# Copied bias rows laid out by partition, and the recurrent parameters loaded as rows and worked out earlier

## The chip, the cores and the metric

The kernel runs on one core of a Trainium2 chip. The metric is the device time of one execution in microseconds (us). Its engines are named as in the profile: PE (TensorE, matrix products; PEld is its weight load), DVE (VectorE), ACT (ScalarE), POOL (GpSimd) and SP (SyncE, which issues the transfers, DMAs). Each engine runs its own instructions in the order in which they were written; the engines wait for each other by semaphores.

## The reference

A row of 256 tokens of width 1024 goes through a first block of two layers and a second block. All is float32.

```python
# first block
for i in range(2):
    h = _multiscale_pool(...) if i == 0 else _diff_attention(...)      # 8 heads, relative position bias
    x = _layernorm(ALPHA * x + h, ...)
    x = _layernorm(ALPHA * x + (silu(x @ w_gate[i]) * (x @ w_up[i])) @ w_down[i], ...)
# second block
proj = rms_norm(x) @ w_in                                              # 1024 x 7752
y_a = moba_attention(...); y_b = dsa_attention(...)                    # 8 heads each, position bias
y_c = rg_lru(causal_depthwise_conv(xc, conv_w, conv_b), w_r, b_r, w_i, b_i, lam) * gelu(yc)
x = x + (sigmoid gates * (y_a @ w_pa, y_b @ w_pb, y_c @ w_pc), summed) @ w_o
x = x + square(relu(rms_norm(x) @ w_up)) @ w_down
return rms_norm(x)
```

The recurrent branch `rg_lru` needs eight vectors of 512 channels (four taps `conv_w`, `conv_b`, `b_r`, `b_i`, `lam`), and of the last one `softplus(-lam)`.

## The kernel before

**Products.** Each float32 operand is split exactly into a high and a low float32r part, and each product is three (high x high, low x high, high x low; lines 304 to 306, helper `mm3`). Weights come by units of 1 MB in two halves of 512 KB (`raw`); ACT casts a half to its high part (line 89), DVE subtracts to get the low part (line 98). Class `Stream` does this in the order of use: five raw halves may be in flight (`RAW_BUFS`), and a half is loaded when DVE has split the half five places before it. `Stream.step` issues such casts and splits after every block of products, so their place in ACT's and DVE's order is fixed when the program is written.

**Side work.** Class `Side` holds chains of short steps (Python generators). `tick`, after each block of 24 or 48 products, issues one step of each active chain, then a step of the stream. The attention heads (`diff_head`) are such chains.

**A feed-forward layer** (`ffn`) runs over eleven chunks of 256 hidden columns. From chunk 2 on a chunk is: 48 products for the gate (`proj_b`), SiLU on ACT (line 558), 48 for `up`, the multiplication on DVE (line 562), the split of the hidden chunk into `hh` (ACT, line 297) and `hl` (DVE, line 298), and then the down projection of the chunk before it into the banks `acc`, 24 products of 512 columns. The last three chunks do only token tile 0 there (12 products); what is due for tile 1 comes in `finish_layer`, which first completes tile 0 (12 products), issues its layer norm, does 24 + 6 products of tile 1 meanwhile, transposes tile 0 into `XTh`/`XTl` (line 373), and does the last 6. Small jobs hang on chunks by number (`aside`, a dictionary: chunk to function), issued after the chunk's products.

**What the change touches.** The position bias of 24 heads is worked out once as a table `R0` in DRAM (24 rows of 383 numbers). `spread_bias(h0)` copies four of these rows 128 times into `Rd` in DRAM, so that `load_bias(h0)` can read, for partition p, the row shifted by p. In the first feed-forward layer chunks 5 and 6 spread heads 0 to 7; in the second one chunks 5 to 8 spread heads 8 to 23. `load_rnn` (second feed-forward layer, chunk 2) loads the eight vectors with channels on partitions, four bytes a piece, into `cw` and `par`; `rnn_params` (chunk 9) works out `softplus(-lam)` by 27 DVE operations and one Exp on ACT, in one go; its results `sp8` are read in the recurrent branch of the second block.

Of the kernel before, what the change touches and what calls it, by code (L numbers as in the profile page):

```python
# [11 lines left out]
F32 = mybir.dt.float32  # L12
# [5 lines left out]
P = 128  # L18
# [19 lines left out]
# the merge of the branches, by blocks of 256 columns: gates (A, B, C), branches (a, b, c), output projection (O)  # L38
# [4 lines left out]
class Stream:  # L43
    """Weights in the order of use: DRAM -> SBUF by halves, each split exactly into a high and a low float32r part."""
# [7 lines left out]
    def load(self, n=None):  # L52
        """Issue loads of halves as far as buffers go, or up to the given count."""
        n = 2 * len(self.units) if n is None else n
        while self.n_dma < min(n, self.n_low + RAW_BUFS):
            i = self.n_dma
            src, (n_k, f) = self.units[i // 2]
            self.raw[i] = self.pool.tile([P, n_k // 2, f], F32, tag="raw", name=f"raw{i}", bufs=RAW_BUFS)
            self.nc.sync.dma_start(self.raw[i], src[:, i % 2 * (n_k // 2):(i % 2 + 1) * (n_k // 2)])
            self.n_dma += 1  # L60
# [42 lines left out]
    def step(self):  # L103
        """The low parts of halves whose high parts an earlier step issued, and the high part of the next half, or of
        two when there is room for two units."""
# [20 lines left out]
class Side:  # L126
    """Chains of short steps, emitted one step each after every block of products, so that their
    latencies pass while the tensor engine works."""
# [4 lines left out]
    def add(self, gen, delay=0, after=(), first=False):  # L133
        """delay: blocks to let pass, once the chains named in after have ended; first: ahead of others"""
# [6 lines left out]
    def tick(self, step=True):  # L141
        """step: of the stream too"""
# [16 lines left out]
def model_kernel(ctx: ExitStack, tc: tile.TileContext, a: dict, out: bass.AP, stop=None):  # L159
# [28 lines left out]
    # ---------------------------------------------------------------- inputs  # L188
# [15 lines left out]
    # -------------------------------------------------------- weight stream  # L204
# [10 lines left out]
    def u_spare(n):  # L215
        """the n-th unit from here goes to buffers that attention leaves free by then"""
        if n is not None:
            spare.add(len(units) + n)
# [42 lines left out]
    # weights of the pooling mix, in a buffer of the stream  # L261
# [17 lines left out]
    # ------------------------------------------------------------ constants  # L279
# [13 lines left out]
    # -------------------------------------------------------------- helpers  # L293
    def split_from(src, h, l, scale=None):
        """h + l = src exactly, both float32r; scale: a power of two or a per-partition column."""
# [12 lines left out]
    def proj_a(o, t, u, tick=True):  # L308
        """o[tok, cols] = X[tile t] @ W"""
# [9 lines left out]
    def proj_b(u, xT=None, n=256):  # L319
        """a bank [cols, j, tok] = (X @ W)^T"""  # L320
# [15 lines left out]
    def down(acc, t, parts, first, last, halves=(0, 1), tick=True):  # L336
        """acc[t][half] += hidden[tile t] @ W rows, for (hidden, unit) in parts"""
# [19 lines left out]
    def rsqrt(v, eps=None):  # L357
        """v[P, n] -> (v + eps) ** -0.5"""
# [21 lines left out]
    def ln(t, acc, g, b, scale=None, first=None, then=None):  # L380
        """first, then: other work, issued where the statistics are waited for"""
# [26 lines left out]
    def rms(t, squares, g):  # L408
        """x * g / rms(x), by halves; squares(h) issues the half's sum of squares and returns its column"""
# [8 lines left out]
    # the end of a layer for one tile: the vector work, then the transposes of the next layer's operand  # L418
# [31 lines left out]
    def finish_out(acc, g, own, late):  # L450
        """own: parts that complete tile 0; late: parts still due for tile 1"""
# [15 lines left out]
    def finish_layer(acc, end, own, late, n_next, quota):  # L467
        """own: parts that complete tile 0; late: parts still due for tile 1. Returns what remains of tile 1's end."""
# [98 lines left out]
    # rows of R0 hold, per head, 8 * bias at distance 255 - j (mask where j > 255); every partition's copy  # L567
    # of them, read at a row pitch one shorter, gives the bias of its query
    R0 = dr.tile([24, NREL], F32, name="R0")
    Rd = dr.tile([24, P, NREL], F32, name="Rd")  # L570
# [32 lines left out]
    def spread_bias(h0):  # L603
        load(Rd[h0:h0 + 4], R0[h0:h0 + 4][:, None, :].to_broadcast([4, P, NREL]))

    def load_bias(h0):
        """[q, head, k] with q of tile 1; columns 128.. serve tile 0"""
        bt = gen("bias", (4, T))
        load(bt, bass.AP(Rd_ap.tensor, Rd_ap.offset + h0 * P * NREL + 127, [[NREL - 1, P], [P * NREL, 4], [1, T]]))
        return bt  # L610

    # --------------------------------------------------- layer 0: pooling mix
    def pool_diff(t, h):
        """a half of (window mean - x)^T"""
# [68 lines left out]
    # ----------------------------------------------------- layer 0: feed forward  # L683
    gb1 = []

    def load_ln(g, b):
# [4 lines left out]
        5: lambda: spread_bias(0), 6: lambda: spread_bias(4)})  # L691
# [3 lines left out]
    # -------------------------------------------- layer 1: differential attention  # L695
# [25 lines left out]
    def proj_t():  # L721
        """a unit's columns, transposed, as float32 in SBUF"""
# [9 lines left out]
    def softmax(qT, kT, j, bias_of, out):  # L732
        """per map c (partitions 64c.. of qT and kT) [q of tile 0 x 128 keys | q of tile 1 x 256 keys]:
        exp(s - max), and the sums, column 2t + c"""
# [22 lines left out]
    def transpose3(src):  # L757
        """[keys, q of tile 0 | q of tile 1] for the first 128 keys, then [keys, q of tile 1] for the others"""
# [45 lines left out]
    v_proj(v, 3, pending)  # L804
    bias = [load_bias(0), load_bias(4)]
# [25 lines left out]
    # ----------------------------------------------------- layer 1: feed forward  # L831
    # parameters of the recurrent branch, channels on partitions: [128, 4]
    cw = sb.tile([P, 4, 4], F32, name="cw")
    par = sb.tile([P, 4, 4], F32, name="par")
    sp8 = sb.tile([P, 3, 4], F32, name="sp8")

    def load_rnn():
        def vec4(w):
            return w.rearrange("(c p) -> p c", p=P)

        for i in range(4):
            load(cw[:, i], vec4(a["conv_w_2"][0, i]))
        for i, n_ in enumerate(("conv_b_2", "b_r_2", "b_i_2", "lru_lambda_2")):
            load(par[:, i], vec4(a[n_][0]))

    def rnn_params():
        # softplus(-lam) = max(-lam, 0) + log1p(e), e = exp(-|lam|); log1p(e) = 2 atanh(e / (2 + e))
        lam = par[:, 3]
        nl, ab, e, z, z2, ser = (small(4) for _ in range(6))
        nc.vector.tensor_scalar_mul(nl, lam, -1.0)  # L850
        nc.vector.tensor_tensor(ab, lam, nl, ALU.min)
        nc.scalar.activation(e, ab, AF.Exp)
        nc.vector.tensor_scalar_add(z, e, 2.0)
        nc.vector.reciprocal(z, z)
        nc.vector.tensor_mul(z, z, e)
        nc.vector.tensor_mul(z2, z, z)
        nc.vector.tensor_scalar(ser, z2, 1.0 / 17.0, 1.0 / 15.0, op0=ALU.mult, op1=ALU.add)
        for d in (13, 11, 9, 7, 5, 3, 1):
            nc.vector.tensor_mul(ser, ser, z2)
            nc.vector.tensor_scalar_add(ser, ser, 1.0 / d)  # L860
        nc.vector.tensor_mul(ser, ser, z)
        nc.vector.tensor_scalar(nl, nl, 0.0, None, op0=ALU.max)
        nc.vector.scalar_tensor_tensor(sp8[:, 0], ser, 2.0, nl, op0=ALU.mult, op1=ALU.add)
        nc.vector.tensor_scalar_mul(sp8[:, 1], sp8[:, 0], -8.0)
# [324 lines left out]
```

## Time and profile before

| | |
|---|---|
| three runs | 991.37, 987.70, 988.67 us; median 988.67 |
| profiled execution | span 989.1 us from first to last instruction; no other time is given for it |
| busy | PE 97%, PEld 90%, DVE 60%, ACT 50%, POOL 2% |
| DMA | 180.81 MB, mean 183 GB/s; 12,386 of 145,611 packets under 512 B |
| six spreads `Rd<-R` | 766 KB each, on SP's queue like all loads |

The span is cut by the profile into 40 slices of 24.7 us. PE's row of busy tenths reads 9 in all of them but three: the first (7), slice 21 (6, from 494.5 us) and the last (7). Slice 21 is the end of the second feed-forward layer. The first feed-forward layer ends at 218.5 us, the first attention runs from there to 330 us, the second feed-forward layer to 534.6 us, then the second block begins. In the rows below, a time in square brackets is how long the engine was idle before that instruction, and the arrow names what ended it.

### The profile page before, as it was taken

To read this page: it belongs to the slowest core of one execution; us is meant where nothing else is said; L and a number is where in the kernel's file an instruction comes from. 1 tells how busy PE (TensorE), PEld (TensorE's weight loads), DVE (VectorE), ACT (ScalarE), POOL (GpSimd) and SP (SyncE) were. 2 spreads that over 40 slices of the span, in tenths; PEclk is the share of its full clock that TensorE was granted. 3 is DMA by queue.
4 is the path that set the end of the run, shared out by engine and by line. 5 is a ranking of instruction groups with operands and counts; after the bars stand their busy time and mean duration, and the time that the engine had idled before them with its cause. 6 is when DMAs were issued, how large, how long until landed. Compare 5 with 4: busy or idle time off the path is not lost.

```text
span 989.1 us, 16902 instructions
## 1 busy us (share of the span) xinstructions
PE 960.2 (97%) x6888; PEld 887.4 (90%) x6888; DVE 590.5 (60%) x970; ACT 495.3 (50%) x817; POOL 21.5 (2%) x45
## 2 busy tenths in 40 slices
PE   7999999999999999999969999999999999999997
PEld 6899999989998898999957999998999999899896
DVE  3774545476577755444547648858845677455553
ACT  3653544355666553434344555669743555344442
POOL 0000000000012000000000000000000000000000
PEclk9999999999999999999988999999999999999999
DMA  8576657656544566765654684452646756565531
GB/s 272 156 253 208 221 173 222 220 162 212 167 143 147 165 213 172 255 212 172 204 176 121 193 242 134 132 168 87 201 160 193 234 172 198 187 221 200 195 107 43
DMA packets 145611, 180.81 MB, mean 183 GB/s; under 512 B 12386, under 2 KB 131419, under 8 KB 145533
## 3 DMA queue, kind: packets, MB, share of 16 engines
q1 hardware_dynamic: 145532, 179.73, 57.1%
q8 instruction: 54, 0.88, 0.4%
q14 instruction: 25, 0.20, 0.1%
HBM read 178.55 MB, written 5.79 MB: 186 GB/s over the span
## 4 chain that ended last, share of the span: by engine, by line
PE 85%; DMA 5%; DVE 5%; ACT 3%; issue 1%; POOL 0%; SPq 0%; POOLq 0%; DVEq 0%; ACTq 0%
PE mm L304 20%; PE mm L306 19%; PE mm L305 19%; PE acc L304 7%; PE acc L305 7%; PE acc L306 7%; DMA raw<-in_w_gate_dram 2%; DVE wl L98 2%; DMA raw<-in_w_down_dram 1%; PE acc L739 1%; ACT wh L89 1%; PE acc L1044 1%; DMA pw<-in_pool_w_dram 1%; PE tr L761 1%; DMA raw<-in_w_up_dram 1%
## 5 line engine op out<-in xcount | busy, mean ns | idle before, releaser
L98 DVE TENSOR_TENSOR wl<-raw,wh 128x1024 fp32r<-128x1024 f32 (+1 forms) x314 | 355.0, 1175 | 104.3 <-ACT wh L89 103.8
L89 ACT CAST wh<-raw 128x1024 fp32r<-128x1024 f32 (+1 forms) x314 | 304.7, 1012 | 191.3 <-issue 100.2
L304 PE MATMUL mm<-XTh,wh 128*128 128x256 f32 x1320 | 373.4, 283 | 0.0
L305 PE MATMUL mm<-XTl,wh 128*128 128x256 f32 x1320 | 369.2, 280 | 0.0
L306 PE MATMUL mm<-XTh,wl 128*128 128x256 f32 x1320 | 368.7, 279 | 0.0
L304 PEld LDWEIGHTS mm<-XTh,wh 128*128 128x128 f32 x1320 | 249.3, 189 | 5.8 <-issue 4.0
L305 PEld LDWEIGHTS mm<-XTl,wh 128*128 128x128 f32 x1320 | 247.3, 187 | 1.2
L306 PEld LDWEIGHTS mm<-XTh,wl 128*128 128x128 f32 x1320 | 247.2, 187 | 0.0
L304 PE MATMUL acc<-wh,hh 128*128 128x512 f32 x352 | 141.4, 402 | 7.0 <-ACT hh L297 7.0
L305 PE MATMUL acc<-wl,hh 128*128 128x512 f32 x352 | 140.2, 398 | 1.5 <-DVE wl L98 1.5
L306 PE MATMUL acc<-wh,hl 128*128 128x512 f32 x352 | 139.1, 395 | 0.0
L304 PEld LDWEIGHTS acc<-wh,hh 128*128 128x128 f32 x352 | 67.0, 190 | 21.7 <-ACT hh L297 8.1
L306 PEld LDWEIGHTS acc<-wh,hl 128*128 128x128 f32 x352 | 67.0, 190 | 17.3 <-DVE hl L298 1.1
L305 PEld LDWEIGHTS acc<-wl,hh 128*128 128x128 f32 x352 | 66.7, 189 | 15.3 <-DVE wl L98 2.3
L298 DVE TENSOR_TENSOR hl<-rn,hh 128x512 fp32r<-128x512 f32 x30 | 20.8, 692 | 89.0 <-ACT hh L297 89.0
L304 PE MATMUL mm<-wh,XTh 128*128 128x256 f32 x256 | 73.5, 287 | 0.2 <-ACT XTh L297 0.2
L305 PE MATMUL mm<-wl,XTh 128*128 128x256 f32 x256 | 72.4, 283 | 1.1 <-DVE wl L98 1.1
L306 PE MATMUL mm<-wh,XTl 128*128 128x256 f32 x256 | 72.4, 283 | 0.5 <-DVE XTl L298 0.5
L305 PEld LDWEIGHTS mm<-wl,XTh 128*128 128x128 f32 x256 | 48.7, 190 | 1.7 <-DVE wl L98 1.6
L306 PEld LDWEIGHTS mm<-wh,XTl 128*128 128x128 f32 x256 | 48.7, 190 | 0.9 <-DVE XTl L298 0.9
L304 PEld LDWEIGHTS mm<-wh,XTh 128*128 128x128 f32 x256 | 48.5, 189 | 1.0 <-ACT XTh L297 0.5
L726 ACT COPY qk<-mm 128x512 f32<-128x512 f32 x22 | 12.9, 587 | 44.9 <-PE mm L306 42.2
(203 smaller groups left out, 894.2 us busy)
## 6 DMA issues: line engine op xcount, KB each, us to landing
raw<-in_w_up_dram SPq DMA_DIRECT2D x76, 512.0 KB, 4.8
raw<-in_w_down_dram SPq DMA_DIRECT2D x76, 512.0 KB, 5.0
raw<-in_w_in_dram SPq DMA_DIRECT2D x60, 512.0 KB, 4.5
raw<-in_w_gate_dram SPq DMA_DIRECT2D x44, 512.0 KB, 7.9
raw<-in_w_qkv_dram SPq DMA_DIRECT2D x24, 512.0 KB, 4.9
raw<-in_w_o_dram SPq DMA_DIRECT2D x16, 512.0 KB, 4.4
Rd<-R SPq DMA_DIRECT2D x6, 766.0 KB
bias<-Rd SPq DMA_DIRECT2D x6, 512.0 KB, 5.2
```

What stands on the lines that cost most here:

```text
L89: self.nc.scalar.copy(h, raw)
L98: self.nc.vector.tensor_sub(l, raw, h)
L298: nc.vector.tensor_sub(l, src, h.bitcast(F32))
L304: nc.tensor.matmul(o, lhsT=lh, rhs=rh, start=first, stop=False)
L305: nc.tensor.matmul(o, lhsT=lh, rhs=rl, start=False, stop=False)
L306: nc.tensor.matmul(o, lhsT=ll, rhs=rh, start=False, stop=last)
L726: nc.scalar.copy(flat(o), b)
L739: nc.tensor.matmul(bs[c][:, SPAN[t]], lhsT=qT[r, j, t * P:(t + 1) * P], rhs=kT[r, j, 0:P * (t + 1)], start=True, stop=True)
L761: nc.tensor.transpose(tb[:, k * P:(k + 1) * P], src[:, k * P:(k + 1) * P], ident)
L1044: nc.tensor.matmul(ob[r, q], lhsT=v[k][:, vc], rhs=pT[c][:, (0, T)[k]:(T, 384)[k]], start=k == 0, stop=k == 1, skip_group_check=True)
```

## The change

`Rd` has the partition as its outermost dimension; the spread writes for each of 128 partitions one run of 4 x 383 numbers, and `load_bias` reads with a row pitch of 24 x 383 - 1 numbers. `load_rnn` now loads the vectors as 32 rows of 128 numbers (five loads), at chunk 7 of the first feed-forward layer. `rnn_params` is a side chain of the first attention: one transpose on PE brings the rows onto partitions, a DVE copy takes them to `rnn`, and the arithmetic, the same, is spread over ten steps. Nothing is left at chunks 2 and 9 of the second layer. (Comments were also removed.)

```diff
-    Rd = dr.tile([24, P, NREL], F32, name="Rd")
+    Rd = dr.tile([P, 24, NREL], F32, name="Rd")
...
     def spread_bias(h0):
-        load(Rd[h0:h0 + 4], R0[h0:h0 + 4][:, None, :].to_broadcast([4, P, NREL]))
+        load(Rd[:, h0:h0 + 4], R0[h0:h0 + 4][None, :, :].to_broadcast([P, 4, NREL]))
     def load_bias(h0):
...
-        load(bt, bass.AP(Rd_ap.tensor, Rd_ap.offset + h0 * P * NREL + 127, [[NREL - 1, P], [P * NREL, 4], [1, T]]))
+        load(bt, bass.AP(Rd_ap.tensor, Rd_ap.offset + h0 * NREL + 127, [[24 * NREL - 1, P], [NREL, 4], [1, T]]))
...
+    rnn_rows = []
+    rnn = sb.tile([P, 8, 4], F32, name="rnn")
+    cw, par = rnn[:, 0:4], rnn[:, 4:8]
+    def load_rnn():
+        rows = gen("gt", (P,))[0:32]
+        rnn_rows.append(rows)
+        load(rows[0:16], a["conv_w_2"][0].rearrange("i (c p) -> (i c) p", p=P))
+        for i, n_ in enumerate(("conv_b_2", "b_r_2", "b_i_2", "lru_lambda_2")):
+            load(rows[16 + 4 * i:20 + 4 * i], a[n_][0].rearrange("(c p) -> c p", p=P))
+    def rnn_params():
+        tb = bank("tr")
+        nc.tensor.transpose(tb[:, 0:32], rnn_rows[0], ident[:32, :32])
+        nc.vector.tensor_copy(rnn.rearrange("p a b -> p (a b)"), tb[:, 0:32])
+        yield
...
+        nc.scalar.activation(e, ab, AF.Exp)
+        yield
...
+        for d in (13, 11, 9, 7, 5, 3, 1):
+            nc.vector.tensor_mul(ser, ser, z2)
+            nc.vector.tensor_scalar_add(ser, ser, 1.0 / d)
+            yield
...
-        5: lambda: spread_bias(0), 6: lambda: spread_bias(4)})
+        5: lambda: spread_bias(0), 6: lambda: spread_bias(4), 7: load_rnn})
...
     v_proj(v, 3, pending)
+    side.add(rnn_params())
     bias = [load_bias(0), load_bias(4)]
...
-    def load_rnn():
-        def vec4(w):
-            return w.rearrange("(c p) -> p c", p=P)
-        for i in range(4):
-            load(cw[:, i], vec4(a["conv_w_2"][0, i]))
-        for i, n_ in enumerate(("conv_b_2", "b_r_2", "b_i_2", "lru_lambda_2")):
-            load(par[:, i], vec4(a[n_][0]))
...
-        2: load_rnn, 3: lambda: load_ln(a["ln_ffn_g"][1], a["ln_ffn_b"][1]),
+        3: lambda: load_ln(a["ln_ffn_g"][1], a["ln_ffn_b"][1]),
...
-        7: lambda: spread_bias(16), 8: lambda: spread_bias(20), 9: rnn_params})
+        7: lambda: spread_bias(16), 8: lambda: spread_bias(20)})
```

On ACT, at the end of the second feed-forward layer, before: `raw_4995` and `raw_5040` are the two halves of the down weights of chunk 9, `hh_5135` is hidden chunk 9, and `rn_5240` is the SiLU of chunk 10.

```order
L89 CAST wh_5132<-raw_4995 128x1024
L89 CAST wh_5132<-raw_5040 128x1024
L297 CAST hh_5135<-rn_5069 128x512
L852 ACT_TABLE_LOAD
L852 ACTIVATE sm_5159<-sm_5158 128x4
L558 ACT_TABLE_LOAD
L558 ACTIVATE rn_5240<-mm_5191 128x512
L89 CAST wh_5243<-raw_5043 128x1024
```

The same place on ACT in the changed kernel (`raw_5029` and `raw_5074` are those two halves now, `hh_5169` is hidden chunk 9):

```order
L89 CAST wh_5166<-raw_5029 128x1024
L89 CAST wh_5166<-raw_5074 128x1024
L297 CAST hh_5169<-rn_5103 128x512
L558 ACTIVATE rn_5240<-mm_5191 128x512
L89 CAST wh_5243<-raw_5077 128x1024
```

Two table loads and the Exp are gone between hidden chunk 9 and the SiLU of chunk 10; the cast of hidden chunk 9 still stands behind both halves of the down weights.

On SP, the last spread and what follows it, before:

```order
L604 DMA Rd<-R_120 512x1x383
L59 DMA raw_4880<-in_w_down_dram 128x1024
L59 DMA raw_4883<-in_w_gate_dram 128x4x256
L59 DMA raw_4941<-in_w_gate_dram 128x4x256
L59 DMA raw_4944<-in_w_up_dram 128x4x256
```

and in the changed kernel:

```order
L604 DMA Rd<-R_120 128x1532
L59 DMA raw_4914<-in_w_down_dram 128x1024
L59 DMA raw_4917<-in_w_gate_dram 128x4x256
L59 DMA raw_4975<-in_w_gate_dram 128x4x256
L59 DMA raw_4978<-in_w_up_dram 128x4x256
```

The spread keeps its place in the queue, ahead of a half of down weights; its rows are 128 of 1532 numbers instead of 512 of 383.

On DVE, at the start of the first attention in the changed kernel (line 787 is the first head's scores, line 746 of the kernel before):

```order
L633 TENSOR_SCALAR sm_2445<-rnn 128x4
L634 TENSOR_TENSOR sm_2446<-rnn,sm_2445 128x4
L637 TENSOR_SCALAR sm_2448<-sm_2447 128x4
L638 RECIPROCAL sm_2448<-sm_2448 128x4
L639 TENSOR_TENSOR sm_2448<-sm_2448,sm_2447 128x4
L640 TENSOR_TENSOR sm_2449<-sm_2448 128x4
L641 TENSOR_SCALAR sm_2450<-sm_2449 128x4
L643 TENSOR_TENSOR sm_2450<-sm_2450,sm_2449 128x4
L644 TENSOR_SCALAR sm_2450<-sm_2450 128x4
L98 TENSOR_TENSOR wl_2454<-raw_2339,wh_2455 128x1024
L98 TENSOR_TENSOR wl_2454<-raw_2372,wh_2455 128x1024
```

These rows are new there but for the two splits; four more follow ahead of the first head's scores, and fourteen between the operations of the first heads, by fours and at the end six.

## Rows read from the trace of the kernel before

**Rows 1.** The page, busy time of PE and its 40 slices.
```profile
PE 960.2 (97%) x6888; PEld 887.4 (90%) x6888; DVE 590.5 (60%) x970; ACT 495.3 (50%) x817; POOL 21.5 (2%) x45
...
PE   7999999999999999999969999999999999999997
```

**Rows 2.** Waits of PE: line, releaser: us in total, times, longest.
```profile
PE acc L304 <- ACT hh L297: 7.0, 2, 5.6
```

**Rows 3.** Timeline of PE, end of the second feed-forward layer: start, us, instruction.
```profile
505.51 0.28 PE L306 MATMUL mm<-XTh,wl 128*128 128x256 f32 x1
507.15 0.50 PE L304 MATMUL acc<-wh,hh 128*128 128x512 f32 x1 [1.36 <-ACT hh L297]
...
518.98 0.79 PE L304 MATMUL acc<-wh,hh 128*128 128x512 f32 x1 [5.61 <-ACT hh L297]
...
532.05 1.31 PE L373 MATMUL tr<-ident,rn 128*128 128x128 f32 x8 [0.41 <-DVE rn L415]
...
534.59 0.28 PE L304 MATMUL mm<-qk,XTh 128*128 128x256 f32 x1
...
536.72 0.39 PE L306 MATMUL mm<-qk,XTl 128*128 128x256 f32 x1 [1.73 <-DVE XTl L298]
```

**Rows 4.** Timeline of PE, end of the first feed-forward layer.
```profile
203.34 0.28 PE L306 MATMUL mm<-XTh,wl 128*128 128x256 f32 x1
...
218.50 0.28 PE L304 MATMUL mm<-wh,XTh 128*128 128x256 f32 x1
```

**Rows 5.** Timeline of ACT, end of the second feed-forward layer.
```profile
505.53 1.04 ACT L89 CAST wh<-raw 128x1024 fp32r<-128x1024 f32 x1 [9.54 <-DMA raw<-in_w_down_dram]
506.48 0.61 ACT L297 CAST hh<-rn 128x512 fp32r<-128x512 f32 x1
...
511.92 0.60 ACT L558 ACTIVATE rn<-mm 128x512 f32<-128x512 f32 x1
```

**Rows 6.** Timeline of DVE there.
```profile
510.01 0.16 DVE L850 TENSOR_SCALAR sm<-par 128x4 f32<-128x4 f32 x1
...
515.21 0.17 DVE L866 TENSOR_SCALAR sp<-sp 128x4 f32<-128x4 f32 x1
...
517.59 0.68 DVE L562 TENSOR_TENSOR rn<-rn,mm 128x512 f32<-128x512 f32 x1
```

**Rows 7.** Timeline of SP: the last spread and the loads behind it.
```profile
490.35 0.62 SPq L604 DMA_DIRECT2D Rd<-R  x1
491.07 6.41 SPq L59 DMA_DIRECT2D raw<-in_w_down_dram  x3
```

**Rows 8.** Windows: length, busy us of five engines, PE's granted clock, DMA share, GB/s.
```profile
434.00:436.00 2.00, 2.00 (x19) 2.00 (x19) 0.00 (x0) 0.44 (x1) 0.00 (x0) 1.00 0.26 94
396.00:402.00 6.00, 6.00 (x52) 5.98 (x51) 2.47 (x3) 2.13 (x3) 0.00 (x0) 1.00 0.95 285
560.00:568.00 8.00, 8.00 (x70) 8.00 (x69) 6.29 (x7) 6.22 (x9) 0.00 (x0) 1.00 0.96 296
510.00:520.00 10.00, 4.25 (x10) 2.52 (x10) 8.94 (x35) 7.61 (x11) 0.00 (x0) 0.54 0.56 170
538.00:542.00 4.00, 4.00 (x23) 4.00 (x22) 3.12 (x9) 1.52 (x4) 0.55 (x1) 0.57 0.28 95
800.00:802.00 2.00, 1.82 (x15) 1.82 (x16) 1.91 (x4) 0.65 (x3) 0.00 (x0) 1.00 0.90 294
```

**Rows 9.** Timeline of DVE, first attention: scores of head 0, then reciprocals of heads 0 and 1.
```profile
252.72 0.29 DVE L746 CUSTOM_DVE_ANT_0 at<-acc,bias 128x128 f32<-128x128 f32 x1 [5.40 <-PE acc L739]
...
259.55 0.18 DVE L771 RECIPROCAL sm<-sm 128x4 f32<-128x4 f32 x1 [3.36 <-ACT at L752]
...
265.21 0.18 DVE L771 RECIPROCAL sm<-sm 128x4 f32<-128x4 f32 x1 [0.47 <-ACT at L752]
...
266.53 0.48 DVE L775 SCALAR_TENSOR_TENSOR at<-at,sm,at 128x256 f32<-128x256 f32 x1
```

**Rows 10.** Timeline of PE, first attention: the transposes that need head 1's result.
```profile
269.99 0.49 PE L761 MATMUL tr<-ident,at 128*128 128x128 f32 x3
```

More of the change, by code (lines that the diff above doesn't have):

```diff
@@ L603, in spread_bias @@
     def spread_bias(h0):
-        load(Rd[h0:h0 + 4], R0[h0:h0 + 4][:, None, :].to_broadcast([4, P, NREL]))
+        load(Rd[:, h0:h0 + 4], R0[h0:h0 + 4][None, :, :].to_broadcast([P, 4, NREL]))
     def load_bias(h0):
         bt = gen("bias", (4, T))
-        load(bt, bass.AP(Rd_ap.tensor, Rd_ap.offset + h0 * P * NREL + 127, [[NREL - 1, P], [P * NREL, 4], [1, T]]))
+        load(bt, bass.AP(Rd_ap.tensor, Rd_ap.offset + h0 * NREL + 127, [[24 * NREL - 1, P], [NREL, 4], [1, T]]))
         return bt
+    rnn_rows = []
+    rnn = sb.tile([P, 8, 4], F32, name="rnn")
+    cw, par = rnn[:, 0:4], rnn[:, 4:8]
+    sp8 = sb.tile([P, 3, 4], F32, name="sp8")
+    def load_rnn():
[9 more added lines that the diff above has]
+        yield
+        lam = par[:, 3]
+        nl, ab, e, z, z2, ser = (small(4) for _ in range(6))
+        nc.vector.tensor_scalar_mul(nl, lam, -1.0)
+        nc.vector.tensor_tensor(ab, lam, nl, ALU.min)
+        nc.scalar.activation(e, ab, AF.Exp)
+        yield
+        nc.vector.tensor_scalar_add(z, e, 2.0)
+        nc.vector.reciprocal(z, z)
+        nc.vector.tensor_mul(z, z, e)
+        nc.vector.tensor_mul(z2, z, z)
+        nc.vector.tensor_scalar(ser, z2, 1.0 / 17.0, 1.0 / 15.0, op0=ALU.mult, op1=ALU.add)
+        for d in (13, 11, 9, 7, 5, 3, 1):
+            nc.vector.tensor_mul(ser, ser, z2)
+            nc.vector.tensor_scalar_add(ser, ser, 1.0 / d)
+            yield
+        nc.vector.tensor_mul(ser, ser, z)
+        nc.vector.tensor_scalar(nl, nl, 0.0, None, op0=ALU.max)
+        nc.vector.scalar_tensor_tensor(sp8[:, 0], ser, 2.0, nl, op0=ALU.mult, op1=ALU.add)
+        nc.vector.tensor_scalar_mul(sp8[:, 1], sp8[:, 0], -8.0)
+        nc.vector.tensor_scalar_mul(sp8[:, 2], sp8[:, 0], -16.0)
+        nc.vector.tensor_scalar_mul(sp8[:, 0], sp8[:, 0], 8.0)
     def pool_diff(t, h):
@@ L829, in model_kernel @@
         return dump()
-    cw = sb.tile([P, 4, 4], F32, name="cw")
-    par = sb.tile([P, 4, 4], F32, name="par")
-    sp8 = sb.tile([P, 3, 4], F32, name="sp8")
-    def load_rnn():
-        def vec4(w):
-            return w.rearrange("(c p) -> p c", p=P)
-        for i in range(4):
-            load(cw[:, i], vec4(a["conv_w_2"][0, i]))
-        for i, n_ in enumerate(("conv_b_2", "b_r_2", "b_i_2", "lru_lambda_2")):
-            load(par[:, i], vec4(a[n_][0]))
[L846 to L864, printed above, removed]
-        nc.vector.tensor_scalar_mul(sp8[:, 2], sp8[:, 0], -16.0)
-        nc.vector.tensor_scalar_mul(sp8[:, 0], sp8[:, 0], 8.0)
     rg = []
     pending = swiglu(2, lambda t, acc: end_ln_rms(t, acc, gb1[-1], rg[0]), pending, 4, 2, {
-        2: load_rnn, 3: lambda: load_ln(a["ln_ffn_g"][1], a["ln_ffn_b"][1]),
+        3: lambda: load_ln(a["ln_ffn_g"][1], a["ln_ffn_b"][1]),
         4: lambda: rg.append(bcast(a["norm_mix_g_2"][0])), 5: lambda: spread_bias(8), 6: lambda: spread_bias(12),
-        7: lambda: spread_bias(16), 8: lambda: spread_bias(20), 9: rnn_params})
+        7: lambda: spread_bias(16), 8: lambda: spread_bias(20)})
     if stop == "ffn1":
```

## The prediction, made before the result was known

> **What bounds the kernel now.** I read the page first: PE is busy 97% of the span, and of its 40 slices only slice 21, besides the first and the last, falls under 9 tenths [rows 1]. So what the change is worth must be looked for in that slice, from 494.5 to 519 us. Next the waits of PE: the longest group is a product in `acc` that waits for ACT's high part of a hidden chunk, 7.0 us in two waits, 5.6 the longest [rows 2]. Then PE's timeline around slice 21, the end of the second feed-forward layer. The last product of the last chunk starts at 505.51, the first of the next layer at 534.59: 29.08 us for 60 products of 512 columns and eight transposes [rows 3]. The first feed-forward layer ends with the same 60 products and eight transposes, and there the same stretch is 218.50 - 203.34 = 15.16 us [rows 4]. The excess is 13.92 us.
>
> Then the timelines of the engines that PE waited for. ACT stood idle 9.54 us until 505.53 for a half of down weights, and only behind that cast does it make hidden chunk 9's high part, at 506.48 [rows 5]; PE's first wait (until 507.15) ends there [rows 3]. That half was issued at 491.07, right behind the last spread at 490.35 [rows 7], so it took 14.4 us. The windows say why: while a spread is alone on the queue the DMA share is 0.26, which is 0.26 x 16 = 4.2 engines, at 94 GB/s; loads of 128 rows show 0.95 and 285 GB/s [rows 8]. A spread's 0.784 MB at 94 GB/s is 8.3 us (an estimate from that row). A weight half has a share on each engine, so it is complete only when its pieces behind the spread on those four are through.
>
> The second cause follows at once: `rnn_params` holds DVE from 510.01 to 515.21 + 0.17 [rows 6], 5.37 us for 27 operations, 0.2 us each, and on ACT it stands ahead of the SiLU of chunk 10, which runs only at 511.92 [rows 5]. So the multiplication of chunk 10 comes at 517.59 [rows 6], and PE, with nothing left to do, waits 5.61 us until 518.98 [rows 3]. Third, the granted clock: 0.54 in the ten us from 510 [rows 8], after PE's waits of 1.36 us (the second of two such stands between the rows shown), so the products around the gap run at the lower of the two levels (1.2 instead of 2.4 GHz).
>
> **The change, part by part.** *The layout of `Rd`.* The spread becomes 128 rows of 6,128 bytes. The nearest rows with that shape, 128 runs that all read one source row, are the `bc` loads in the window 396 to 402 (together with weight halves): 0.95, 285 GB/s [rows 8]. At that rate the spread takes 0.784 / 0.285 = 2.75 us, on all engines, instead of 8.3 on four. From the other side, if it stayed as it is, the cost is unchanged (a rival, below). I take 2.75, since the row count and not the direction is what the change alters. The down half behind the last spread would then land some 5 to 8 us earlier, before 500, when hidden chunk 9 is not yet wanted: PE first asks for it at 505.63.
>
> The Trainium skill, page "DMA: Bandwidth & Descriptors", section "Why a DMA increments its semaphore by 16 and not by 1", says that the number of engines is the largest number up to 16 that divides the slowest dimension of both sides. By that rule four heads outermost would give the four engines that the windows show, and 128 rows would give 16. No run before shows a copy from DRAM to DRAM on 16; by the rule the sum below holds, by the spreads' own row alone it would be that of the first rival.
>
> The three earlier spreads of that layer cost PE nothing (its slices read 9 [rows 1]), nor do the two in the first layer, so shortening those gains nothing on the path.
>
> *`rnn_params` away from chunk 9.* DVE loses 5.37 us there and ACT two table loads and an Exp. With the first part alone DVE would do them at about 497, under 96 products of chunk 10, so the two parts largely overlap: either takes most of the second wait, the layout also the first.
>
> *`rnn_params` in the first attention.* 28 operations of DVE, 28 x 0.2 = 5.6 us, in steps. Thirteen and the copy come ahead of the scores of head 0, before which DVE idles 5.40 us for PE, and four ahead of its reciprocals, where it idles 3.36 us for ACT: hidden. Four (0.8 us) come ahead of head 1's reciprocals, where it idles only 0.47 us: 0.33 us late [rows 9]. What waits for those is PE's transposes at 269.99 [rows 10]; their input is done at 266.53 + 0.48 = 267.01 [rows 9], so 3 us of slack covers it. The last six (1.2 us) delay only the normalization of head 0, used one block later. Cost zero; without that cover, at most 1.2 us. The Exp brings no table load of its own, since the heads' Exp needed it anyway. PE gains one transpose, under the 1.31 / 8 = 0.16 us of a full one [rows 3]: 0.1. Its result goes through one of the two `tr` banks, unused at that time.
>
> *`load_rnn`.* Five issues of SP at 0.62 us [rows 7], 3 us, stand ahead of a half of down weights in chunk 7 of the first layer. Five halves are in flight there and PE never waits; the spread before it is now shorter by more. Zero; if the cover were gone, 3 us. The eight old loads stood under a busy PE: no gain. *`load_bias`* keeps its 128 x 4 rows of 1 KB; only the pitch grows to 36,764 bytes. Loads of `w_in` read 1 KB runs at a pitch of 31,008 bytes at 0.96 and 296 GB/s [rows 8]: zero.
>
> *What is late next.* The end of this layer has an RMS norm behind the layer norm, which the first one has not. Its transposes wait 0.41 us and the first low part of the next layer 1.73 us, behind three weight splits in DVE's order [rows 3]. Both stay. In the changed kernel DVE comes to tile 0's sums straight from five splits and the chunk's own work, so I add 0.3 us to the first. At 538 to 542 the clock is at 0.57 [rows 8]: (1 - 0.57) x 4 = 1.7 us lost after those waits. Whether that returns I can't tell: after a wait in the second block of 2.00 - 1.82 = 0.18 us it stayed at 1.00 [rows 8]. I take half, 0.85 us gained, and keep 0 and 1.7.
>
> **Sum.** 13.92 - 0.41 - 0.3 + 0.85 - 0.1 = 13.96 us gained. The profile's span is 989.1, 0.4 above the median of 988.67; the gain from the median gives **974.7 us**.
>
> **Rivals.** *The spread stays on four engines* (the change doesn't do what it says): for it, no copy within DRAM here runs on more; against it, every load with 128 rows does [rows 8]. Then the half still comes at 505.53, and only `rnn_params` is gone: the SiLU moves from 511.92 to 507.1, when the hidden chunk's cast ends (506.48 + 0.61 [rows 5]), 4.8 us, and DVE has 5.37 us less. The smaller counts: 989.1 - 4.8 = 984.3, 983.9 from the median.
>
> *A new wait takes the old one's place.* On ACT seven casts of weights stand between the SiLU of chunk 10 and hidden chunk 10's high part, one of them of a half of `w_in` that is loaded only when the stream's splits allow. If that holds up PE by 2.5 us, the clock falls again: at half speed 12 products of 0.23 us, about (15.16 / 66) each [rows 4], lose 2.8 us. 974.7 + 5.3 = 980.0. Against it: the first layer's end has the same order and lost nothing [rows 4].
>
> *Slower: the bias rows read slowly.* If a pitch of 36,764 bytes made `load_bias` run as the spreads do, 94 instead of 296 GB/s [rows 8], a pair of 1.05 MB would take 11.2 instead of 3.5 us and hold up the weights behind it by 7.7; there are three pairs. 974.7 + 3 x 7.7 = 997.8. It decides from 14 / 3 = 4.7 us a pair on that nothing covers. The `w_in` row speaks against it.
>
> **Chances.** The forecast 0.77 (its own range 971.5 to 977.5: both waits and the clock gone, or 1.2 in the attention and no clock gain), the new wait 0.10, four engines 0.08, slow bias rows 0.05. The range 970.5 to 981.5 takes in the forecast and the new wait, 0.87, less what falls outside at its ends. A measurement of this kernel tells 0.5%, 4.9 us, from no change: faster is the forecast and the new wait, 0.87; same is four engines, 0.08, as 983.9 is 4.8 below; slower 0.05.
>
> **What would show it.** In the profile of the changed kernel slice 21 of PE reads 9. ACT no longer waits some 9 us for down weights ahead of hidden chunks; a window with a spread shows a DMA share near 1. The stretch from the last product of chunk 10 to the next layer's first is 15.5 to 16 us, with the clock at 1.00 in it. PE's waits of 0.4 to 0.8 and 1.7 us stand right behind. The first attention has no new wait of PE. Wrong: a DMA share of 0.26 in a spread, a wait of PE in `acc` for ACT at the layer's end, or PE waiting between 230 and 310 us.

## The result and the profile after

The changed kernel takes 979.07 us (median of 4 runs, 977.52 to 980.36) against 989.86 for the kernel before in the same comparison: a ratio of 0.9892, 95% interval 0.9877 to 0.9907, 10.8 us gained. Two repeats gave 978.42 (0.9874, 0.9849 to 0.9899) and 979.09 (0.9897, 0.9877 to 0.9917). The forecast was 974.7, range 970.5 to 981.5: the direction and the range hold, and the gain, 13.96 us by the sum, came out some 3 us smaller. The forecast's own range, 971.5 to 977.5, does not hold.

The page of the profiled run (977.52 us, span 975.6): busy time of PE, its 40 slices and its granted clock. It answers to [rows 1].

```profile
PE 957.0 (98%) x6889; PEld 885.8 (91%) x6889; DVE 590.6 (61%) x971; ACT 491.8 (50%) x815; POOL 21.5 (2%) x45
...
PE   8999999999999999999998999999999999999997
...
PEclk8999999999999999999999999999999999999999
```

The 6 in slice 21 is gone; the 8 that is left beside it, in slice 22, takes in the end of the layer and the start of the next. Of PE's waits (line, releaser: us in total, times, longest), the first group of [rows 2], `acc` for ACT's `hh`, no longer exists:

```profile
PE tr L661 <- DMA x<-in_x_dram: 4.5, 1, 4.5
PE mm L306 <- DVE XTl L298: 2.1, 3, 1.7
PE tr L802 <- DVE at L816: 1.3, 2, 0.9
```

PE's timeline at the end of the second feed-forward layer, for [rows 3] (start, us, instruction, idle time before it and what ended it):

```profile
505.62 0.28 PE L306 MATMUL mm<-XTh,wl 128*128 128x256 f32 x1
505.74 0.39 PE L304 MATMUL acc<-wh,hh 128*128 128x512 f32 x1
...
518.82 1.32 PE L373 MATMUL tr<-ident,rn 128*128 128x128 f32 x8 [0.34 <-DVE rn L415]
...
521.36 0.28 PE L304 MATMUL mm<-qk,XTh 128*128 128x256 f32 x1
...
523.49 0.38 PE L306 MATMUL mm<-qk,XTl 128*128 128x256 f32 x1 [1.73 <-DVE XTl L298]
```

Read the first and the last `mm` around the transposes: 521.36 - 505.62 = 15.74 us, where it was 29.08, and 15.16 in the first layer [rows 4]. The only gap left in it is the 0.34 ahead of the transposes. The windows (length, five engines, granted clock, DMA share, GB/s) show the last spread with loads around it, and the clock of the stretch:

```profile
484.00:488.00 4.00, 4.00 (x37) 4.00 (x35) 0.26 (x2) 1.81 (x3) 0.00 (x0) 1.00 0.91 356
505.00:522.00 17.00, 16.41 (x78) 12.95 (x76) 13.71 (x24) 8.50 (x15) 1.09 (x2) 1.00 0.48 148
```

A DMA share of 0.91 and 356 GB/s where [rows 8] has 0.26 and 94 for a spread alone, and a clock of 1.00 where it had 0.54. ACT's timeline answers to [rows 5]:

```profile
491.77 2.00 ACT L89 CAST wh<-raw 128x1024 fp32r<-128x1024 f32 x2 [3.09 <-issue]
493.68 0.62 ACT L297 CAST hh<-rn 128x512 fp32r<-128x512 f32 x1
500.28 0.60 ACT L558 ACTIVATE rn<-mm 128x512 f32<-128x512 f32 x1 [5.99 <-PE mm L306]
...
506.82 0.61 ACT L297 CAST hh<-rn 128x512 fp32r<-128x512 f32 x1
```

No cast waits for `w_down` any more. Hidden chunk 9's high part is ready at 494.3, eleven us before PE wants it, and the SiLU of chunk 10 waits for PE instead of keeping it waiting. SP's timeline, for [rows 7], and DVE's, for [rows 6]:

```profile
480.84 0.48 SPq L604 DMA_DIRECT2D Rd<-R  x1
482.92 6.42 SPq L59 DMA_DIRECT2D raw<-in_w_down_dram  x3
```

```profile
505.93 0.69 DVE L562 TENSOR_TENSOR rn<-rn,mm 128x512 f32<-128x512 f32 x1 [1.72 <-PE mm L306]
...
519.34 3.49 DVE L98 TENSOR_TENSOR wl<-raw,wh 128x1024 fp32r<-128x1024 f32 x3
522.75 1.28 DVE L298 TENSOR_TENSOR XTl<-tr,XTh 128x512 fp32r<-128x512 f32 x2
```

The product of chunk 10 stands at 505.93 instead of 517.59, and the three splits ahead of `XTl` still make PE's 1.73 us. In the first attention [rows 9, 10] PE has one new row, and no wait that it didn't have:

```profile
239.80 0.24 PE L627 MATMUL tr<-ident,gt 32*128 32x32 f32 x1
...
311.55 0.30 PE L802 MATMUL tr<-ident,at 128*128 128x128 f32 x1 [0.88 <-DVE at L816]
```

### The profile page after: what moved, and what is told of

Read it like the earlier page. It is cut to its first block, busy times and chain, and to the rows that moved or that the text cites. A ratio compares the mean times of both kernels' runs of the same rounds, so it can differ in the third digit from the quotient of the medians.

```text
span 975.6 us, 16904 instructions
## 1 busy us (share of the span) xinstructions
PE 957.0 (98%) x6889; PEld 885.8 (91%) x6889; DVE 590.6 (61%) x971; ACT 491.8 (50%) x815; POOL 21.5 (2%) x45
## 4 chain that ended last, share of the span: by engine, by line
PE 91%; DVE 4%; ACT 3%; issue 1%; POOL 0%; DMA 0%; POOLq 0%; SPq 0%; DVEq 0%; ACTq 0%
PE mm L304 21%; PE mm L306 20%; PE mm L305 20%; PE acc L305 8%; PE acc L304 8%; PE acc L306 8%; DVE wl L98 1%; PE acc L780 1%; PE acc L1050 1%; PE tr L802 1%; PE tr L373 1%; ACT rn L378 1%; ACT wh L89 1%; POOL sm L365 0%; DVE x L389 0%
## 5 line engine op out<-in xcount | busy, mean ns | idle before, releaser
L304 PEld LDWEIGHTS mm<-XTh,wh 128*128 128x128 f32 x1320 | 246.7, 187 | 5.9 <-issue 4.0
L304 PE MATMUL acc<-wh,hh 128*128 128x512 f32 x352 | 139.4, 396 | 0.0
L558 ACT ACTIVATE rn<-mm 128x512 f32<-128x512 f32 x18 | 10.8, 600 | 60.7 <-PE mm L306 60.7
```

What stands on the lines that cost most here:

```text
L304: nc.tensor.matmul(o, lhsT=lh, rhs=rh, start=first, stop=False)
L558: nc.scalar.activation(s, b, AF.Silu)
```

## The experiments

Each ran beside the kernel before on its chip; ratios carry 95% intervals. To compare whole profiles I cut each one at the first transpose (L373) into the operand of the next stage. That splits off what varies from run to run at the start. All parts in us:

```
                  until   first  first    second  mixers,  MLP,
                  first   FF     attn.    FF      merge    end
before             22.2   194.0  113.6    202.2   265.2    191.9
before_again       23.4   194.9  113.5    199.7   264.8    191.9
rnn_only           24.0   195.1  113.9    199.4   264.9    191.8
spread_early       20.5   194.7  113.5    194.9   264.7    191.7
wide16             24.3   195.1  114.0    190.5   264.9    191.6
changed            20.4   195.2  114.0    189.2   265.0    191.8
after_again        23.3   195.3  113.9    189.3   265.0    191.7
after_third        24.0   195.2  114.0    189.2   264.8    191.8
loads4             24.0   195.1  113.6    189.3   264.9    191.8
layout_only        21.0   194.8  113.5    188.8   264.8    191.8
order_only         21.4   194.8  113.7    188.8   264.7    191.9
order_again        23.2   194.9  113.6    188.8   264.7    191.9
quota0             23.7   195.2  114.0    189.2   267.9    191.8
quota1             23.6   195.1  113.9    189.3   268.9    191.7
```

**The two halves of the change, each alone.** layout_only is the kernel before with the new `Rd`, spread and `load_bias` (the first three changed places of the change's diff), and `rnn_params` left at chunk 9.

> The kernel before with the new layout of the copied bias rows alone; the parameters are loaded and worked out as before, at chunks 2 and 9. Theory (the late half of down weights is the first cause, and without it the small operations of chunk 9 run under the 96 products of chunk 10): no wait of PE in acc at the end of the second feed-forward layer, time within 1.5 us of the changed kernel, 977 to 981. Rival (the small operations and table loads are the cause, the layout only adds to it): a wait of PE of 4 us or more for ACT remains there, time 983 to 987.

Measured: 979.45 us, 0.9883 (0.9859 to 0.9906); the second layer takes 188.8 us, and no wait for `hh` is left. DVE, then PE, at the layer's end:

```profile
496.58 0.16 DVE L850 TENSOR_SCALAR sm<-par 128x4 f32<-128x4 f32 x1
...
505.30 0.69 DVE L562 TENSOR_TENSOR rn<-rn,mm 128x512 f32<-128x512 f32 x1 [1.05 <-PE mm L306]
```

```profile
518.14 1.32 PE L373 MATMUL tr<-ident,rn 128*128 128x128 f32 x8 [0.40 <-DVE rn L415]
520.71 0.28 PE L304 MATMUL mm<-qk,XTh 128*128 128x256 f32 x1
```

So the layout alone takes everything, although the parameters' 27 small operations still stand at chunk 9: they now run from 496.58 on, under the products of chunk 10, and the multiplication of that chunk waits for PE.

rnn_only is the changed kernel with the old layout and spread (those three places put back).

> The changed kernel with the old layout of the copied bias rows: only the parameters are moved. Theory: the down half behind the last spread still lands 14 us after its issue, PE's first wait (until hidden chunk 9) stays and the second shrinks by some 5 us: about 4.8 us below before, 983 to 987, and the clock falls to half again. Rival (the small operations were the cause): within 1.5 us of the changed kernel.

Measured: 989.81 us, 0.9994 (0.9978 to 1.0010): nothing gained, against both sizes expected. PE's timeline at the layer's end:

```profile
509.07 0.28 PE L306 MATMUL mm<-XTh,wl 128*128 128x256 f32 x1
510.14 0.51 PE L304 MATMUL acc<-wh,hh 128*128 128x512 f32 x1 [0.80 <-ACT hh L297]
512.01 0.51 PE L305 MATMUL acc<-wl,hh 128*128 128x512 f32 x1 [1.36 <-DVE wl L98]
...
519.96 0.80 PE L304 MATMUL acc<-wh,hh 128*128 128x512 f32 x1 [4.71 <-ACT hh L297]
...
534.91 0.28 PE L304 MATMUL mm<-qk,XTh 128*128 128x256 f32 x1
```

and ACT's, which says why the second wait is still there:

```profile
508.53 1.05 ACT L89 CAST wh<-raw 128x1024 fp32r<-128x1024 f32 x1 [9.51 <-DMA raw<-in_w_down_dram]
509.48 0.61 ACT L297 CAST hh<-rn 128x512 fp32r<-128x512 f32 x1
510.00 0.59 ACT L558 ACTIVATE rn<-mm 128x512 f32<-128x512 f32 x1
...
515.72 1.14 ACT L89 CAST qk<-raw 128x512 fp32r<-128x512 f32 x2 [2.21 <-DMA raw<-in_w_in_dram]
518.35 1.04 ACT L89 CAST wh<-raw 128x1024 fp32r<-128x1024 f32 x1 [1.49 <-DMA raw<-in_w_in_dram]
519.30 0.61 ACT L297 CAST hh<-rn 128x512 fp32r<-128x512 f32 x1
```

The SiLU does come right behind `hh`, as foretold. But the casts ahead of chunk 10's `hh` now wait 2.21 and 1.49 us for halves of `w_in`. Two halves of `w_in` were issued only at 512.02 and 513.15, because the splits that free their buffers had been standing behind the late down half, until 510.74. The lateness passed through the stream into the next loads.

**Is the 29.08 us typical?** before_again is the kernel before, unchanged.

> The kernel before, unchanged, for a second profile of its stretch at the end of the second feed-forward layer beside the one that the prediction was read from. If the 29.08 us there are typical of it, the last product of chunk 10 and the first of the next layer stand 28 to 30 us apart again, with a wait of 5 to 6 us for the multiplication of chunk 10 in it, and then parameters alone (rnn_only, which took 25.7 us there in its profile, and no less time in all) really shortened the stretch by some 3 us and lost them elsewhere. Rival: the stretch varies by several us from run to run (down to 25 or 26); then rnn_only changed nothing at all there. Ratio 1.00 within 0.3%.

Measured: 988.73 us, 0.9988 (0.9974 to 1.0002). PE's timeline:

```profile
507.53 0.28 PE L306 MATMUL mm<-XTh,wl 128*128 128x256 f32 x1
507.65 0.39 PE L304 MATMUL acc<-wh,hh 128*128 128x512 f32 x1
509.27 0.50 PE L305 MATMUL acc<-wl,hh 128*128 128x512 f32 x1 [1.23 <-DVE wl L98]
...
519.24 0.80 PE L304 MATMUL acc<-wh,hh 128*128 128x512 f32 x1 [6.71 <-ACT hh L297]
...
534.05 0.28 PE L304 MATMUL mm<-qk,XTh 128*128 128x256 f32 x1
```

26.52 us, not 29.08: the rival holds. One 30 us window over the end of the layer, first of the kernel before as profiled for the prediction, then of before_again, shows where the difference lies:

```profile
505.00:535.00 30.00, 21.09 (x77) 14.94 (x76) 22.89 (x56) 17.48 (x27) 1.10 (x2) 0.77 0.42 134
```

```profile
505.00:535.00 30.00, 20.93 (x94) 15.71 (x93) 23.44 (x56) 17.46 (x27) 1.09 (x2) 0.89 0.45 139
```

With two levels, 2.4 and 1.2 GHz, a mean of 0.77 is 2 x 0.23 x 30 = 13.8 us at the lower one, and 0.89 is 6.6. The waits are nearly equal (1.36 + 1.36 + 0.16 + 5.61 + 0.41 = 8.90 and 1.23 + 0.17 + 6.71 + 0.40 = 8.51 us); the rest, 2.2 us, is left to the products that ran at the lower clock for longer. rnn_only has 0.89 there as well, so its fair partner is before_again: 25.84 against 26.52 us, 0.7 gained and lost in the noise of the times.

**Four engines: layout, order or run length?** wide16 takes rnn_only, and in place of four spreads of 4 heads it makes one of 16 at chunk 5, layout and 1,532-byte runs as before (`spread_bias` takes the number of heads as a second argument):

```diff
...
-5: lambda: spread_bias(8), 6: lambda: spread_bias(12), 7: lambda: spread_bias(16), 8: lambda: spread_bias(20)
+5: lambda: spread_bias(8, 16)
...
```

> rnn_only's order of the parameters with the old layout (heads outermost) and one spread of 16 heads at chunk 5 in place of four spreads of 4 heads at chunks 5 to 8: the same bytes, the same 1,532-byte runs. Theory (the number of engines follows the outermost dimension): with 16 rows outermost it runs on all engines, DMA share about 0.9 or more for some 8 to 11 us, nothing is late at the layer's end, and the time is within 3 us of the changed kernel's (976 to 982). Rival A (1,532-byte runs within DRAM are slow themselves, or a copy in this direction goes on four engines): the share is 0.26 for some 33 us and the time is that of rnn_only or above (988 or more). Rival B (all engines, but packets of about 10 us each as before keep the queue for longer than the buffers cover): share 0.9, but a wait of PE around chunk 6; 981 to 987.

Measured: 981.03 us, 0.9903 (0.9888 to 0.9918). A window inside the spread:

```profile
440.00:456.00 16.00, 16.00 (x115) 14.93 (x114) 3.05 (x3) 2.92 (x3) 0.00 (x0) 1.00 1.10 175
```

All engines are busy (the share counts packets by their times, so it can pass 1), at 175 GB/s instead of 94. So rival A falls. The time, 981.03, lies in the theory's band (976 to 982) and in rival B's (981 to 987), and the profile has some of both: one spread of 3.14 MB takes 20.3 us (first to last packet) instead of the 8 to 11 expected (the 10 us that the expectation gives a packet are those of a spread; a packet took 0.07 us before), ACT waits 13.11 us for the down half behind it, and PE waits 0.48 + 0.17 us at chunk 6.

order_only changes one line of the kernel before. `Rd` keeps heads outermost, and the spread walks the destination by partitions:

```diff
-        load(Rd[h0:h0 + 4], R0[h0:h0 + 4][:, None, :].to_broadcast([4, P, NREL]))
+        load(Rd[h0:h0 + 4].rearrange("h p n -> p h n"), R0[h0:h0 + 4][None, :, :].to_broadcast([P, 4, NREL]))
```

> The kernel before with one line changed: Rd keeps its layout (heads outermost), and the spread names its destination partition first, 128 rows of four runs of 1,532 bytes, in place of 512 rows. The bytes lie where they lay and load_bias is as before; only the order in which the copy walks is new, and rnn_params stays at chunk 9. Theory (what counts is the outermost dimension of the copy, not the layout): the spreads run on all engines, about 5 us each (the 16-head spread took 20.3 us for four times the bytes), nothing is late at the layer's end, the stretch there is 15.7 to 16.5 us, and the time is that of the changed kernel, 977 to 981. Rival A (the rows must be contiguous over heads, 6,128 bytes, as the new layout makes them): the spreads take 10 us as before, and the time is before's, 988 to 991. Rival B (all engines, but short runs hold the queue too long near the end): 5 us each, yet a wait of PE of 1 to 3 us remains at the layer's end; 981 to 985.

Measured: 976.61 us, 0.9868 (0.9851 to 0.9885); again, below, 977.95. The layer's end, PE and the window of the last spread:

```profile
518.73 1.32 PE L373 MATMUL tr<-ident,rn 128*128 128x128 f32 x8 [0.40 <-DVE rn L415]
521.29 0.28 PE L304 MATMUL mm<-qk,XTh 128*128 128x256 f32 x1
523.39 0.38 PE L306 MATMUL mm<-qk,XTl 128*128 128x256 f32 x1 [1.71 <-DVE XTl L298]
```

```profile
484.00:488.00 4.00, 4.00 (x36) 4.00 (x36) 0.28 (x1) 1.84 (x3) 0.00 (x0) 1.00 0.70 230
```

The theory stands, rivals A and B fall: the second layer takes the same 188.8 us as with the new layout, the stretch at its end is 15.73 us, and the only waits of PE about it are those of the changed kernel. It isn't where the bytes lie that counts, it is which dimension the copy names first.

**Only the end, or wherever the cover ends?** spread_early is the kernel before, with the four spreads at chunks 2 to 5 in place of 5 to 8.

> The kernel before, with its layout and its chunk 9, but the four spreads of the second feed-forward layer at chunks 2 to 5 instead of 5 to 8. Each still runs on four DMA engines. Theory (only the spreads near the layer's end matter, as the stretch of chunks between takes up the lateness): no wait of PE in acc at the end, 977 to 981. Rival (spreads on four engines cost by adding up, wherever they stand): less than half of the gain, 985 or more.

Measured: 984.41 us, 0.9937 (0.9915 to 0.9959), about half of the gain: under neither of the two as they were put. The layer's end is clean, but SP's timeline, with the last two of the four spreads, and PE's have this at chunk 6:

```profile
423.63 0.61 SPq L604 DMA_DIRECT2D Rd<-R  x1
...
445.01 0.62 SPq L604 DMA_DIRECT2D Rd<-R  x1
```

```profile
441.30 0.50 PE L304 MATMUL acc<-wh,hh 128*128 128x512 f32 x1 [1.25 <-ACT hh L297]
443.16 0.50 PE L305 MATMUL acc<-wl,hh 128*128 128x512 f32 x1 [1.36 <-DVE wl L98]
```

PE waits here behind the third spread, before the fourth is issued. ACT's waits for the down weights behind the four were 5.09, 10.76, 10.01 and 8.97 us; behind PE's waits the clock is at half for 3.4 us. (Chunks 2 to 4 also hold the small loads of that layer; what they add was not tried by itself.)

In the kernel before, ACT's waits behind the four spreads of this layer were 3.28, 6.57, 9.03 and 9.54 us, each on top of the delay that the last one left:

```profile
445.48 1.05 ACT L89 CAST wh<-raw 128x1024 fp32r<-128x1024 f32 x1 [3.28 <-DMA raw<-in_w_down_dram]
...
465.61 1.05 ACT L89 CAST wh<-raw 128x1024 fp32r<-128x1024 f32 x1 [6.57 <-DMA raw<-in_w_down_dram]
...
485.34 1.05 ACT L89 CAST wh<-raw 128x1024 fp32r<-128x1024 f32 x1 [9.03 <-DMA raw<-in_w_down_dram]
```

SP came to the first spread of this layer at 430.26 us before and 430.21 after, and to the fourth at 490.35 and 480.84: 9.5 us of delay had gathered ahead of it. The two spreads of the first layer made ACT wait 3.12 and 5.75 us, and PE not at all. So spreads on four engines do add up, and PE waits where the sum exceeds what the buffers cover: after the fourth in the kernel before, after the third here.

**What the moved parameters cost.** loads4 is the changed kernel with the old eight loads of 4-byte pieces in chunk 7 of the first layer, without the transpose and its copy.

> The changed kernel, with the recurrent parameters loaded as before (eight loads of 4-byte pieces, 4,096 pieces in all, straight to channels on partitions), at the place of the new load in chunk 7 of the first feed-forward layer, and without the transpose and its copy. If the way in which these parameters are loaded costs nothing either way there, as the prediction put it, the time is within 1.5 us of the changed kernel's. Rival: the small pieces hold the queue up by several us, and PE waits for a half of down weights near the end of the first feed-forward layer: 2 to 8 us slower than the changed kernel.

Measured: 978.71 us, 0.9880 (0.9861 to 0.9898): no different in time. In the table its first attention takes 113.6 us, that of the kernels with the transpose 113.9 to 114.0. Then the one-line version beside the changed kernel on one chip:

> The one-line version (before's layout and order of work, the spread's destination walked partition first) again, on the same chip as the changed kernel. In the profiles taken so far, from the first transposes of layer 0 (at 20 to 24 us) to the end, it took 953.9 us and the changed kernel 955.2; the parts with the parameters moved are longer by 0.2 to 0.5 us each, at four places, in every profile that has them. Theory: that is the cost of the moved parameters (a transpose, five loads, the steps in the attention), and the one-line version is 0.8 to 1.8 us faster in the median. Rival: the two are equal within 0.5 us, and what the profiles show is chance.

Measured: 977.95 us (976.27 to 979.31), 0.9883 (0.9862 to 0.9904), and the changed kernel, as after_third, 979.09 (977.43 to 980.95), 0.9897. The medians differ by 1.14 us, but the runs overlap, so the times alone don't settle it. On another chip layout_only took 979.45 and the changed kernel 978.42, the other way round. The profiles agree better: from the first transposes to the end the one-line version took 953.9 us both times, the changed kernel 955.2, 955.2 and 955.0. Some 1.2 us goes with the moved parameters: 0.4 in the first attention, 0.3 in the first layer, 0.4 in the second. Only the first of these has a place: 0.25 us of it comes at the new transpose, and loads4, which lacks the transpose and its copy, lacks the 0.4. In the first layer PE falls behind evenly, from long before the new loads (161 us), and in the second, where nothing of the parameters is left, evenly too; no wait shows it. What makes these two stays open.

**A version that beats both?** The 1.73 us for `XTl` stand behind three weight splits on DVE. quota0 and quota1 allow none or one of the two halves that the stream may split ahead (`finish_layer`'s quota 2 to 0, to 1).

> The changed kernel, with no weight splits allowed while the second feed-forward layer ends (finish_layer's quota 0 in place of 2), so that fewer splits of the next weights stand on DVE ahead of XTl's low part. If PE's wait of 1.73 us for XTl is made by those three splits, it falls to 0.5 or less, and the time to 976 to 978, 1 to 2 us under the changed kernel in these runs. Rival: the splits are only put off, PE waits as long for them some products later (a wait of 1.5 us or more for a weight part in the next projection), and the time is within 0.5 us of the changed kernel's or over it.

Measured: 981.22 us, 0.9909 (0.9893 to 0.9925). XTl's wait is gone; some 5 and 8 us behind its place PE has:

```profile
532.27 0.38 PE L304 MATMUL mm<-wh,XTh 128*128 128x256 f32 x1 [1.81 <-ACT wh L89]
534.79 0.43 PE L305 MATMUL mm<-wl,XTh 128*128 128x256 f32 x1 [2.15 <-DVE wl L98]
```

> The changed kernel with finish_layer's quota 1 in the second feed-forward layer: one of the three weight splits that stand on DVE ahead of XTl's low part moves behind it. With quota 0 all are put off, and PE's 1.73 us for XTl turned into 1.81 and 2.15 us for weight parts. If there is a middle way, XTl's wait falls to 0.5 us (1.73 less one split of 1.2) and the later waits stay under 0.5: 0.7 to 1.2 us under the changed kernel's time. Rival: the weight parts are wanted within the next unit of products, so what is put off is waited for in full there: waits of 0.5 and 1.2 us or more, no gain or a loss of up to 1.5 us.

Measured: 980.63 us, 0.9913 (0.9895 to 0.9931), with waits of 0.60, 0.66 and 2.14. Neither gains: against the kernel before on their chip they take 9.0 and 10.1 us less, the changed kernel 9.6 to 11.4. What is put off is waited for in full, and behind it more. In their profiles the clock also falls to half behind these waits, for 3.4 and 6.8 us, and the part that begins there (mixers, merge) is longer by 2.9 and 3.9 us; but these two executions, 983.71 and 984.33 us, stand at the upper end of their six, so that loss is not typical. The best version measured is order_only, one line, level with or a little ahead of the changed kernel.

## Why the prediction was right, and where it was off

*The spread's four engines were the cause, and the layout removed it.* Right, and more so than said: layout_only has the whole gain. It was not the layout as such, though: order_only has the gain with the old one. The rival that the spread stays on four engines is excluded: of its own packets up to 18 are under way at once, mostly 4 or fewer before. Its price, 983.9, would have been wrong too: rnn_only is that case, at 989.81.

*"The three earlier spreads of that layer cost PE nothing", so shortening them gains nothing.* The second half of this is wrong. PE did not wait behind them, but their delays had gathered in the stream (9.5 us at the fourth spread), and without them the fourth would hold ACT up by some 3 us, as the first did without a wait of PE (an estimate from the first spread's 3.28). The sum did not suffer, since the change shortens all of them. A spread before took 9.6 to 10.7 us, not the 8.3 of the estimate.

*"Either takes most of the second wait."* This step failed for the parameters. Taking 4.8 us from ACT's order and 5.37 from DVE's was counted as a gain of the smaller; of PE's waits (8.51 in before_again, 7.43 in rnn_only) 1.1 us went, and of the time nothing that could be measured. The late down half had a second way to the same wait, through the buffers of the stream to the loads of `w_in`. It didn't show in the profile before, since the parameters' own delay lay over it.

*The excess of 13.92 us.* This is the term that was mis-sized. It was right for the one profile, and the stretch afterwards, 15.74, fell into the 15.5 to 16 foretold. But 29.08 was a profile with 13.8 us of lower clock; the second one has 6.6 and 26.52. That the span stood only 0.4 from the median hid this, for two oddities cancelled: the same profile has full clock in its first 40 us, where every other shows 3.4 to 10.2 us of half speed, and reached the first attention at 216.2 us, before_again at 218.3.

*The clock behind the 1.73 us wait, 0.85 gained.* Wrong by the same cause: before_again has a clock of 1.00 from 535 to 545 behind the same wait, so there was nothing to regain. *The 0.3 added to the RMS wait*: it came out at 0.34, less than the 0.41 before. *Zero for the first attention and 0.1 for the transpose*: no wait of PE is new there, but the part is longer by 0.4 to 0.5 us.

With these sizes the sum is 13.96 - 2.56 - 0.85 + 0.37 - 0.35 = 10.6 us, or 9.9 with the 0.3 and 0.4 of the two feed-forward layers that no term foresaw; the three comparisons gave 10.8, 11.4 and 9.6. *The rival of a new wait on ACT* named 980.0, nearer to the measured time than the forecast's 974.7, but its mechanism isn't in the changed kernel: hidden chunk 10's `hh` came at 506.82 without holding PE. (It is in rnn_only, where ACT does wait for halves of `w_in`.) That the measured time still fell into the range was in part luck: 977.5 to 981.5 was there for this rival. *Slow bias rows* didn't happen: at the two loads whose landing both traces show, `load_bias` took 7.1 and 5.6 us with the new layout (layout_only) and 6.7 and 5.6 with the old one (order_only), and the part that uses it takes 265.0 us in the changed kernel against 264.8 and 265.2 before.

## What to carry to other kernels

When one queue feeds everything, look at the DMA share of each kind of transfer by itself. A copy that sits on a few engines is paid by the loads behind it, chunks later and on another engine's wait; naming the larger dimension first can be the whole repair. Before a stretch of a single profile is taken as the price, look whether its clock is that of a second profile: the waits repeat, the half-speed time around them need not. And removing the last of several delays in a chain pays only if the one below it is gone too.

## What the runs showed of the hardware

From the start of its first packet to the start of its last one in the traces' records, a spread of 0.784 MB took 9.6 to 10.7 us in the kernel before, 4.8 to 6.4 us in order_only (same 1,532-byte packets, partitions first) and 3.2 to 5.0 us in the changed kernel (6,128-byte packets). So the order of walking is worth a factor of two, and the longer run the rest, which the kernel's time doesn't show; the sum's 2.75 us, taken from loads of 128 rows, was too short for a copy within DRAM. The Trainium skill, page "DMA: Bandwidth & Descriptors", section "Why a DMA increments its semaphore by 16 and not by 1", takes the largest number of engines up to 16 that divides the slowest dimension of both sides. Here 4, 16 and 128 outermost gave DMA shares of 0.26, 1.10 and 0.70 to 0.91 (the last three with other loads beside them), and of the spread's own packets 4 were under way at once for most of the time and 7 at the most with 4 outermost, up to 22, 20 and 18 in wide16, order_again and the changed kernel: this case agrees.

By the same records a 1,532-byte packet took 71 ns on the mean (36.2 us over 512) in the kernel before, 86 to 103 in order_only, and 139 (284 us over 2,048) in wide16. The median is 65 in order_only and 109 in wide16, so in order_only some packets are much longer and most are not. Whether the other loads under way make them so was not tried.

The clock falls to half for 3.4 to 10.2 us in the first 40 us of every profile but one, and the part until the first transposes takes 20.4 to 24.3 us without regard to the kernel. That spread is as large as the runs' own, and the cause stays open.
